# Scan outputs of all token tiles in two PSUM banks, one for each half of the heads

## The chip, the core and the metric

The kernel runs on one core of a Trainium2 chip. What counts is the device time of one execution in microseconds. TensorE (PE in the profile) multiplies matrices into PSUM, VectorE (DVE), ScalarE (ACT) and GpSimd (POOL) work element by element, SyncE (SP) issues most transfers, and the DMA engines move data between HBM and SBUF.

## The reference

The model is a backbone of two layers over 256 context tokens and 256 latent tokens, 1024 features wide. Each layer has a token mixer of four head groups (A windowed attention, B neighbourhood attention, C a gated convolution, D a gated linear recurrence that runs in both directions) and then an expert layer, which fills most of the time. The change touches only the output of group D. Its reference goes chunk by chunk:

```
attn = jnp.einsum('bhid,bhjd,bhijd->bhij', qc, kc, decay)
o = jnp.einsum('bhij,bhjv->bhiv', attn, vc) + jnp.einsum('bhid,bhdv->bhiv', qc * jnp.exp(G), S)
...
return o_f + rev(o_b), oc_f + rev(oc_b)
```

So an output is a product inside the chunk (attention weights by values) plus, for each direction, a decayed query times the state that the chunk starts from. There are four heads of 64 features.

## The kernel before

Tokens lie in four tiles of 128: tiles 0 and 1 are context, 2 and 3 latent. Layer 0 works on all four, layer 1 (the last one) mixes only the latent tiles. In group D the feature-major operands hold two heads on the 128 partitions: index ct chooses the pair of heads, hh the half of the partitions (0 to 63 or 64 to 127) on which a head lies.

The mixer of a layer is a list of named pieces, ORDERS (L58), and the function mixers runs them in that order (L856). The pieces that matter here:
- d_level:n (L740, hgrn_level) computes one level of the in-chunk weights: ScalarE, GpSimd and VectorE build operands, TensorE multiplies them into two "sc" banks, one for each half (L547), and VectorE merges them into attnT (L554). d_states (hgrn_states) carries the states from chunk to chunk: transposes (L484), products (L490), VectorE updates (L497, L500).
- d_out (L745) makes the outputs. For each token tile tt and half hh, hgrn_out's inner function o (L560) takes the one buffer with tag "o", adds for both ct the in-chunk term (128 rows deep, attnT by di) and the state terms (64 rows deep, eG by st), and VectorE copies the 128x128 result into yd (L751). Layer 0 has eight such results, layer 1 four.
- b_v, b_k, b_q, d_gate are projections: in_slab loads a weight slab, splits it into a high and a low part (L211 or L213, and L215), and mm3 (L224) runs three matmuls for each block of 128 input features. proj and wide take the result bank with tag "mm", of which there are three (self.nmm).
- a_attn:tt and b_attn:tt are attention pieces: scores in "sc" (L597), transposes in "tr" (L618), outputs in "o" (L622).

PSUM has eight banks: "sc" 2, "tr" 2, "mm" 3, "o" 1. The order written in the list is not the order on the engines: a scheduler moves instructions ahead where their operands and buffers allow. The buffers of a tag are given out in program order, so the n-th user of "mm" waits for the release of the buffer by the user three before it. In the list of layer 0 stands 'a_attn:0', 'b_q', 'd_out', 'a_attn:2', 'b_v', 'b_k'; in that of layer 1 'd_level:6', 'd_out', 'b_k', 'd_gate', 'b_v', 'b_q'. An fp32 matmul is two records in the trace.

Of the kernel before, what the change touches and what calls it, by code (L numbers as in the profile page):

```python
# [15 lines left out]
AF = mybir.ActivationFunctionType  # L16
# [5 lines left out]
P = 128  # L22
# [162 lines left out]
class Kernel:  # L185
# [370 lines left out]
    def hgrn_out(self, at, di, dirs, psp):  # L556

        nc = self.nc

        def o(tt, hh):  # L560
            po = self.t(psp, [P, 2, 64], tag="o", bufs=1)
            c = slice(tt * P, tt * P + P)
            r = slice(hh * 64, hh * 64 + 64)
            for ct in range(2):
                h = ct * 2 + hh
                terms = [(at[:, hh, tt, ct, :], di[:, tt, h * 64:h * 64 + 64])]
                for states, e in dirs:
                    if tt in states:
                        terms.append((e[r, ct, c], states[tt][r, ct, :]))
                for m, (x, y) in enumerate(terms):  # L570
                    nc.tensor.matmul(po[:, ct, :], x, y, start=m == 0, stop=m == len(terms) - 1)
            return po
        return o

    def attention(self, name, l, qT, kx, kc, v, heads, tt, y, pool, psp, mask=None, sink=None):

# [77 lines left out]
    def mixers(self, l, modt, tick=None, pre=()):  # L654
        nc, A, tc = self.nc, self.A, self.tc
        V, S, Gp = nc.vector, nc.scalar, nc.gpsimd
        last = l == DEPTH - 1
        lo = C if last else 0
        tts = list(range(lo // P, 4))
        with ExitStack() as es:  # L660
            fp = es.enter_context(tc.tile_pool(name=f"fp{l}", bufs=1))
            psp = es.enter_context(tc.tile_pool(name=f"ps{l}", bufs=2, space=PSUM))
# [48 lines left out]
            b = _Bag()  # L711
# [31 lines left out]
                self.hgrn_level(n, b.at, l, b.q, b.kd, b.Gd, fp, psp)  # L743

            def d_out():  # L745
                of = self.hgrn_out(b.at, b.di, [b.states[0], b.states[1]], psp)
                b.yd = self.t(fp, [P, 4, 256], tag="yd")
                for tt in tts:
                    yv = b.yd[:, tt, :].rearrange("p (c h d) -> p h c d", c=2, h=2)
                    for hh in range(2):  # L750
                        V.tensor_copy(yv[:, hh], of(tt, hh))  # L751

            def d_gate():
                for n, ps in enumerate(wide("dg", lo)):
# [101 lines left out]
            for piece in ORDERS[l]:  # L856
                name, _, d = piece.partition(":")
# [605 lines left out]
```

## Time and profile before

| | us |
|---|---|
| three timed runs, median | 2888.43 |
| lowest and highest | 2881.9, 2890.88 |
| the profiled execution | 2893.59 |
| its span in the trace | 2891.8 |
| TensorE busy | 2716.0 (94%) |
| VectorE busy | 2072.2 (72%) |
| ScalarE busy | 1142.5 (40%) |
| GpSimd busy | 1102.7 (38%) |
| mean granted TensorE clock | 0.967 |

The mixers run in two stretches of the span, layer 0 early (scan levels and outputs around 150 to 270 us) and layer 1 around 1800 to 1950 us. The output matmuls are at 225 to 246 us and at 1875 to 1890 us. A share of the whole span says little about them, so the rows below are taken from these stretches. [...] Matmuls overlap: one matmul's record is longer than the distance to the next, so paces are read from starts.

### The profile page before, as it was taken

To read this page: it belongs to the slowest core of one execution; us is meant where nothing else is said; L and a number is where in the kernel's file an instruction comes from. 1 tells how busy PE (TensorE), PEld (TensorE's weight loads), DVE (VectorE), ACT (ScalarE), POOL (GpSimd) and SP (SyncE) were. 2 spreads that over 40 slices of the span, in tenths; PEclk is the share of its full clock that TensorE was granted. 3 is DMA by queue.
4 is the path that set the end of the run, shared out by engine and by line. 5 is a ranking of instruction groups with operands and counts; after the bars stand their busy time and mean duration, and the time that the engine had idled before them with its cause. 6 is when DMAs were issued, how large, how long until landed. Compare 5 with 4: busy or idle time off the path is not lost.

```text
span 2891.8 us, 41509 instructions
## 1 busy us (share of the span) xinstructions
PE 2716.0 (94%) x15750; PEld 2398.9 (83%) x15750; DVE 2072.2 (72%) x3616; ACT 1142.5 (40%) x1742; POOL 1102.7 (38%) x651
## 2 busy tenths in 40 slices
PE   7799999889999999999999988999889999999998
PEld 4678788779999898888887867689889998887776
DVE  6883878999677888888878867747973315665655
ACT  4433433235533333333333334334345544444443
POOL 3531134455145344433433304425656574440000
PEclk9988999999999999999999998989999999999999
DMA  6321423347889899999989952324557776557884
GB/s 237 110 81 58 127 88 117 97 157 270 296 281 332 317 336 333 333 338 329 326 319 351 370 169 86 98 85 151 158 186 241 245 248 228 183 189 260 277 275 162
DMA packets 265784, 639.24 MB, mean 221 GB/s; under 512 B 19184, under 2 KB 136688, under 8 KB 262768
## 3 DMA queue, kind: packets, MB, share of 16 engines
q1 hardware_dynamic: 228720, 502.36, 51.4%
q0 software_dynamic: 36864, 134.23, 12.6%
q8 instruction: 123, 2.02, 0.3%
q14 instruction: 77, 0.63, 0.1%
HBM read 574.39 MB, written 62.13 MB: 220 GB/s over the span
## 4 chain that ended last, share of the span: by engine, by line
PE 32%; DVE 25%; DMA 18%; issue 9%; ACT 4%; POOL 2%; DVEq 0%; ACTq 0%; POOLq 0%; SPq 0%
DMA wraw<-in_uT_dram 12%; PE S L224 11%; PE mm L224 8%; DVE vL L215 7%; DMA ga<-spd 5%; PE pa L1307 5%; PE G L1197 5%; ACT ah L1257 2%; DVE ga L1254 2%; ACT wH L211 2%; DVE t L1046 1%; DVE wL L215 1%; DVE eq L939 1%; DVE al L1261 1%; DVE tok L1064 1%
## 5 line engine op out<-in xcount | busy, mean ns | idle before, releaser
L215 POOL TENSOR_TENSOR wL<-wraw,wH 128x1024 fp32r<-128x1024 f32 x228 | 577.3, 2535 | 739.7 <-ACT wH L211 542.7
L224 PE MATMUL S<-hH,wL 128*128 128x384 f32 (+1 forms) x2048 | 606.2, 314 | 20.6 <-POOL wL L215 13.3
L224 PE MATMUL S<-hH,wH 128*128 128x384 f32 (+1 forms) x2048 | 605.7, 314 | 5.0 <-ACT wH L211 3.2
L211 ACT ACTIVATE wH<-wraw 128x1024 fp32r<-128x1024 f32 x320 | 337.2, 1055 | 395.9 <-DMA wraw<-in_uT_dram 359.5
L224 PEld LDWEIGHTS S<-hH,wL 128*128 128x128 f32 x2048 | 393.4, 192 | 31.1 <-POOL wL L215 14.5
L1307 PE MATMUL pa<-vH,al 128*128 128x512 f32 x1280 | 399.2, 393 | 19.4 <-DVE al L1261 19.2
L224 PEld LDWEIGHTS S<-hH,wH 128*128 128x128 f32 x2048 | 393.1, 192 | 10.6 <-ACT wH L211 5.7
L1307 PE MATMUL pa<-vL,ah 128*128 128x512 f32 x1280 | 396.9, 391 | 3.2 <-DVE vL L215 2.9
L1307 PE MATMUL pa<-vH,ah 128*128 128x512 f32 x1280 | 395.6, 390 | 2.5 <-ACT ah L1257 1.8
L215 DVE TENSOR_TENSOR vL<-wraw,vH 128x1024 fp32r<-128x1024 f32 x256 | 333.3, 1332 | 66.1 <-ACT vH L211 64.8
L224 PE MATMUL S<-hL,wH 128*128 128x384 f32 (+1 forms) x2048 | 348.2, 311 | 0.0
L211 ACT ACTIVATE vH<-wraw 128x1024 fp32r<-128x1024 f32 x256 | 263.3, 1053 | 186.4 <-PE pa L1307 144.1
L224 PEld LDWEIGHTS S<-hL,wH 128*128 128x128 f32 x2048 | 312.7, 191 | 0.0
L1307 PEld LDWEIGHTS pa<-vH,al 128*128 128x128 f32 x1280 | 237.5, 188 | 81.5 <-DVE al L1261 34.0
L1013 POOL DMA_INDIRECT row<-in_v_dram,idx x128 | 188.3, 1471 | 301.9 <-DVE tok L1064 277.3
L1307 PEld LDWEIGHTS pa<-vL,ah 128*128 128x128 f32 x1280 | 238.8, 188 | 59.1 <-DVE vL L215 10.0
L1013 POOL DMA_INDIRECT row<-in_u_dram,idx x128 | 180.9, 1413 | 270.6 <-DVE score L1046 230.0
L1307 PEld LDWEIGHTS pa<-vH,ah 128*128 128x128 f32 x1280 | 238.2, 188 | 48.9 <-ACT ah L1257 2.2
L224 PE MATMUL mm<-hH,wH 128*128 128x256 f32 (+1 forms) x776 | 256.1, 349 | 9.9 <-ACT hH L362 2.5
L224 PE MATMUL mm<-hH,wL 128*128 128x256 f32 (+1 forms) x776 | 252.4, 344 | 8.6 <-DVE wL L215 8.3
L1109 ACT ACTIVATE ga<-S 128x384 f32<-128x384 f32 (+1 forms) x256 | 110.4, 432 | 332.0 <-PE S L224 331.5
L1261 DVE TENSOR_TENSOR al<-ga,ah 128x768 fp32r<-128x768 f32 (+1 forms) x128 | 137.4, 1074 | 138.0 <-ACT ah L1257 138.0
(322 smaller groups left out, 4076.4 us busy)
## 6 DMA issues: line engine op xcount, KB each, us to landing
wraw<-in_uT_dram SPq DMA_DIRECT2D x256, 512.0 KB, 4.4
wraw<-in_v_dram SPq DMA_DIRECT2D x256, 512.0 KB, 5.7
gd<-gst SPq DMA_DIRECT2D x20, 2048.0 KB, 6.7
wraw<-in_w_in_dram SPq DMA_DIRECT2D x52, 512.0 KB, 3.6
gt<-gd SPq DMA_DIRECT2D x32, 768.0 KB, 9.4
row<-in_w_modT_dram SPq DMA_DIRECT2D x48, 512.0 KB, 6.6
wraw<-in_w_modT_dram SPq DMA_DIRECT2D x32, 512.0 KB, 3.7
wraw<-in_w_q_dram SPq DMA_DIRECT2D x32, 512.0 KB, 3.7
```

The lines of the kernel that those rows point to most:

```text
L211: nc.scalar.activation(h, w, AF.Copy)
L215: e.tensor_tensor(lo, w, h.bitcast(F32), op=ALU.subtract)
L224: nc.tensor.matmul(ps, x, y, start=start and m == 0, stop=stop and m == len(seq) - 1, skip_group_check=skip)
L939: V.tensor_tensor(eq, self.iota16.unsqueeze(1).unsqueeze(1).to_broadcast(shape), rank.unsqueeze(3).to_broadcast(shape), op=ALU.is_equal)
L1013: Gp.indirect_dma_start(out=x, out_offset=None, in_=rows[n], in_offset=bass.IndirectOffsetOnAxis(ap=idx[:, k:k + 1], axis=0))
L1046: V.tensor_tensor_reduce(j, x, ht, 1.0, 0.0, op0=ALU.mult, op1=ALU.add, accum_out=a[:, k:k + 1])
L1109: self.gelu = S.activation(ga[:, e, :], ps, AF.Gelu_apprx_tanh)
L1197: nc.tensor.matmul(pg[:, t, :], Y[:, q + t, :], X[:, q + t, :], start=True, stop=True)
L1254: V.tensor_tensor(gv, gv, b.gt[:, :, g % 2 * 2:g % 2 * 2 + 2].rearrange("p b e t -> p e b t"), op=ALU.mult)
L1257: S.activation(b.ah, ga, AF.Copy)
L1261: V.tensor_tensor(b.al, b.gated, b.ah.bitcast(F32), op=ALU.subtract)
L1307: nc.tensor.matmul(pacc[tau, h], (ah, ah, al)[m][:, e, tau * P:(tau + 1) * P], vs[e][m == 1][:, h * 512:h * 512 + 512], start=g == 0 and e ...
```

## The change

Function o now takes a token tile alone. Two buffers for the whole piece, one for each half of the heads, hold the results of all four token tiles ([P, 4, 2, 64] in fp32, one bank each). They come from the tag "mm". Inside, the two halves alternate: the in-chunk terms of both halves, then for each direction the state terms of both halves. After all tiles one ScalarE instruction copies half 0 and one VectorE instruction half 1 into yd.

```diff
--- before.py
+++ after.py
@@ -557,20 +557,21 @@
 
         nc = self.nc
 
-        def o(tt, hh):
-            po = self.t(psp, [P, 2, 64], tag="o", bufs=1)
+        def o(tt):
             c = slice(tt * P, tt * P + P)
-            r = slice(hh * 64, hh * 64 + 64)
             for ct in range(2):
-                h = ct * 2 + hh
-                terms = [(at[:, hh, tt, ct, :], di[:, tt, h * 64:h * 64 + 64])]
-                for states, e in dirs:
-                    if tt in states:
-                        terms.append((e[r, ct, c], states[tt][r, ct, :]))
-                for m, (x, y) in enumerate(terms):
-                    nc.tensor.matmul(po[:, ct, :], x, y, start=m == 0, stop=m == len(terms) - 1)
-            return po
-        return o
+                live = [(states[tt], e) for states, e in dirs if tt in states]
+                for hh in range(2):
+                    h = ct * 2 + hh
+                    nc.tensor.matmul(po[hh][:, tt, ct, :], at[:, hh, tt, ct, :], di[:, tt, h * 64:h * 64 + 64], start=True,
+                                     stop=not live)
+                for m, (st, e) in enumerate(live):
+                    for hh in range(2):
+                        r = slice(hh * 64, hh * 64 + 64)
+                        nc.tensor.matmul(po[hh][:, tt, ct, :], e[r, ct, c], st[r, ct, :], start=False,
+                                         stop=m == len(live) - 1)
+        po = [self.t(psp, [P, 4, 2, 64], tag="mm", bufs=self.nmm) for _ in range(2)]
+        return o, po
 
     def attention(self, name, l, qT, kx, kc, v, heads, tt, y, pool, psp, mask=None, sink=None):
 
@@ -743,12 +744,14 @@
                 self.hgrn_level(n, b.at, l, b.q, b.kd, b.Gd, fp, psp)
 
             def d_out():
-                of = self.hgrn_out(b.at, b.di, [b.states[0], b.states[1]], psp)
+                of, po = self.hgrn_out(b.at, b.di, [b.states[0], b.states[1]], psp)
                 b.yd = self.t(fp, [P, 4, 256], tag="yd")
                 for tt in tts:
-                    yv = b.yd[:, tt, :].rearrange("p (c h d) -> p h c d", c=2, h=2)
-                    for hh in range(2):
-                        V.tensor_copy(yv[:, hh], of(tt, hh))
+                    of(tt)
+                c = slice(tts[0], 4)
+                yv = b.yd.rearrange("p t (c h d) -> p h t c d", c=2, h=2)
+                S.activation(yv[:, 0, c], po[0][:, c], AF.Copy)
+                V.tensor_copy(yv[:, 1, c], po[1][:, c])
 
             def d_gate():
                 for n, ps in enumerate(wide("dg", lo)):
```

How the order on TensorE changes at three places. Numbers after a name are running numbers of buffers.

Layer 0, in the scan levels (about 175 us). mm_1673 is a result bank of b_v, tr and sc are the states' and levels' banks. Before:

```order
L224 MATMUL mm_1673<-wL_1664,hH_290 128x256
L547 MATMUL sc_1157<-big_1141,big_1140 128x128 x3
L547 MATMUL sc_1158<-big_1141,big_1140 128x128 x3
L547 MATMUL sc_1157<-big_1141,big_1140 128x128
L547 MATMUL sc_1158<-big_1141,big_1140 128x128
L484 MATMUL tr_1214<-small_59,big_1183 128x128 x2
L224 MATMUL mm_1673<-wL_1670,hH_290 128x256 x4
L490 MATMUL tr_1219<-di_589,khT_1217 128x128
```

After, at the same place:

```order
L547 MATMUL sc_1157<-big_1141,big_1140 128x128 x3
L547 MATMUL sc_1158<-big_1141,big_1140 128x128 x3
L547 MATMUL sc_1157<-big_1141,big_1140 128x128
L547 MATMUL sc_1158<-big_1141,big_1140 128x128
L490 MATMUL tr_1193<-di_589,khT_1191 128x128 x2
L484 MATMUL tr_1201<-small_59,big_1183 128x128 x2
L547 MATMUL sc_1169<-big_1141,big_1140 128x128 x3
L547 MATMUL sc_1170<-big_1141,big_1140 128x128 x3
```

b_v's matmuls (L224) no longer stand between those of the levels; its first one stands behind the first two of d_out (L566 into mm_1526 and mm_1527).

Layer 0, d_out. o_1551 is the one output buffer, mm_1836 a projection's bank. Before, one result:

```order
L571 MATMUL o_1551<-di_589,attnT_893 128x64
L571 MATMUL o_1551<-st_1209,eG_1181 128x64
L571 MATMUL o_1551<-st_1374,eG_1333 128x64
L571 MATMUL o_1551<-di_589,attnT_893 128x64
L571 MATMUL o_1551<-st_1209,eG_1181 128x64
L571 MATMUL o_1551<-st_1374,eG_1333 128x64
L224 MATMUL mm_1836<-hH_290,wH_1832 128x512
L224 MATMUL mm_1836<-hH_290,wL_1833 128x512
```

After, from the middle of d_out; mm_1526 holds half 0 and mm_1527 half 1:

```order
L566 MATMUL mm_1526<-di_589,attnT_893 128x64
L566 MATMUL mm_1527<-di_589,attnT_893 128x64
L571 MATMUL mm_1526<-st_1209,eG_1181 128x64
L571 MATMUL mm_1527<-st_1209,eG_1181 128x64
L571 MATMUL mm_1526<-st_1374,eG_1333 128x64
L571 MATMUL mm_1527<-st_1374,eG_1333 128x64
L566 MATMUL mm_1526<-di_589,attnT_893 128x64
L566 MATMUL mm_1527<-di_589,attnT_893 128x64
```

The halves alternate between two banks, all of d_out but its first two matmuls is in one piece without projection matmuls in it, and the 'a_attn:2' transposes and outputs and the rest of b_v and all of b_k stand behind it.

Layer 1, b_k. mm_15748 is b_k's first bank, sc_15378 and sc_15379 belong to a level, sc_15397 to attention. Before, in the levels:

```order
L224 MATMUL mm_15748<-hH_14553,wH_15744 128x512
L224 MATMUL mm_15748<-hH_14553,wL_15745 128x512
L224 MATMUL mm_15748<-hH_14553,wH_15744 128x512
L224 MATMUL mm_15748<-hH_14553,wL_15745 128x512
L547 MATMUL sc_15378<-dq_15002,big_15375 128x128 x4
L224 MATMUL mm_15748<-hL_14554,wH_15744 128x512 x2
L547 MATMUL sc_15379<-dq_15002,big_15375 128x128 x4
L597 MATMUL sc_15397<-ak_15140,aq_15067 128x512
L224 MATMUL mm_15748<-hL_14554,wH_15744 128x512 x3
```

After, the end of d_out (mm_15696 is half 0, mm_15697 half 1) and the first matmuls of b_k (mm_15732):

```order
L566 MATMUL mm_15697<-di_14753,attnT_15228 128x64
L571 MATMUL mm_15697<-st_15328,eG_15287 128x64
L571 MATMUL mm_15696<-st_15648,eG_15620 128x64
L571 MATMUL mm_15697<-st_15648,eG_15620 128x64
L566 MATMUL mm_15696<-di_14753,attnT_15228 128x64
L566 MATMUL mm_15697<-di_14753,attnT_15228 128x64
L571 MATMUL mm_15696<-st_15328,eG_15287 128x64
L571 MATMUL mm_15697<-st_15328,eG_15287 128x64
L571 MATMUL mm_15696<-st_15648,eG_15620 128x64
L571 MATMUL mm_15697<-st_15648,eG_15620 128x64
L224 MATMUL mm_15732<-hH_14541,wH_15728 128x512
L224 MATMUL mm_15732<-hH_14541,wL_15729 128x512
```

All of b_k's 48 matmuls of 512 columns, and 21 of the gate's, which were spread over the levels, now stand behind d_out. In d_out itself the two halves alternate only in the last eight matmuls; ahead of these come runs with one half alone, in which 128-row and 64-row terms follow one another. On VectorE two weight steps of b_k's second slab (L213, L215), which stood between the state updates, stand behind the output copy, and two group-norm steps of A (L637) stand ahead of it.

## Rows read from the trace of the kernel before

**Rows 1.** Page, part 1: busy us, share of the span, instructions of each engine.

```profile
PE 2716.0 (94%) x15750; PEld 2398.9 (83%) x15750; DVE 2072.2 (72%) x3616; ACT 1142.5 (40%) x1742; POOL 1102.7 (38%) x651
```

**Rows 2.** Stretches in layer 0: length, busy PE, PEld, DVE, ACT, POOL, PEclk, DMA share, GB/s.

```profile
172.00:195.00 23.00, 21.41 (x176) 18.98 (x174) 20.54 (x36) 4.73 (x8) 6.55 (x4) 0.95 0.19 58
195.00:224.00 29.00, 29.00 (x165) 20.34 (x164) 26.91 (x63) 13.67 (x36) 4.02 (x3) 1.00 0.49 155
...
242.00:257.00 15.00, 15.00 (x59) 13.19 (x58) 1.01 (x3) 1.20 (x2) 0.00 (x0) 0.52 0.00 1
257.00:270.00 13.00, 11.69 (x36) 6.73 (x36) 4.09 (x12) 5.09 (x13) 3.42 (x3) 0.64 0.26 81
```

**Rows 3.** PE groups by form, 171.9 to 195 us: busy us, mean ns, idle before.

```profile
L224 PE MATMUL mm<-wH,hH 128*128 128x256 f32 x23 | 6.1, 296 | 0.0
...
L224 PE MATMUL mm<-wL,hH 128*128 128x256 f32 x16 | 2.7, 293 | 0.0
```

**Rows 4.** Stretches in layer 1, columns as in rows 2.

```profile
1818.00:1842.00 24.00, 21.14 (x119) 14.16 (x117) 23.28 (x53) 5.27 (x10) 13.42 (x17) 0.93 0.39 125
1842.00:1875.00 33.00, 30.97 (x225) 24.00 (x221) 21.48 (x56) 17.65 (x44) 13.89 (x28) 1.00 0.14 46
1875.00:1890.00 15.00, 15.00 (x64) 13.23 (x64) 2.51 (x7) 1.06 (x1) 0.00 (x0) 0.58 0.05 20
1895.00:1911.00 16.00, 16.00 (x136) 15.87 (x134) 5.83 (x8) 5.60 (x13) 5.77 (x4) 1.00 0.40 125
```

**Rows 5.** PE groups by form, 1818.5 to 1874.9 us, columns as in rows 3.

```profile
L224 PE MATMUL mm<-hH,wH 128*128 128x512 f32 x16 | 7.3, 454 | 0.0
...
L224 PE MATMUL mm<-wH,hH 128*128 128x256 f32 x8 | 2.1, 296 | 0.0
```

**Rows 6.** Who waited for the output matmuls of line 571: us, times.

```profile
  DVE yd L751: 25.5, 12
```

**Rows 7.** ACT groups by form, 225 to 260 us, columns as in rows 3.

```profile
L620 ACT ACTIVATE PT<-tr 128x512 f32<-128x512 f32 x4 | 2.4, 598 | 20.7 <-PE o L622 18.9 <-PE tr L618 1.8
```

**Rows 8.** Chain of waits, 1868 to 1912 us: start, us, what.

```profile
1869.71 0.69 DVE wH L213
...
1871.69 1.22 DVE wL L215
...
1874.99 0.80 PE o L571 x4
...
1890.39 20.64 PE mm L224 x155
1911.03 1.05 PE sc L597 x3
```

**Rows 9.** Timeline of PE, 237.9 to 247 us: start, us, instructions.

```profile
237.91 0.33 PE L571 MATMUL o<-di,attnT 128*128 128x64 f32 x2
238.17 0.66 PE L571 MATMUL o<-st,eG 64*128 64x64 f32 x4
238.75 0.43 PE L571 MATMUL o<-di,attnT 128*128 128x64 f32 x2
239.12 0.66 PE L571 MATMUL o<-st,eG 64*128 64x64 f32 x4
239.70 0.50 PE L224 MATMUL mm<-hH,wH 128*128 128x512 f32 x1
...
244.02 1.11 PE L571 MATMUL o<-st,eG 64*128 64x64 f32 x4
245.06 0.69 PE L571 MATMUL o<-di,attnT 128*128 128x64 f32 x2
245.68 1.11 PE L571 MATMUL o<-st,eG 64*128 64x64 f32 x4
```

**Rows 10.** Chain of waits, 1828 to 1831 us, columns as in rows 8.

```profile
1829.74 1.10 PE sc L547 x16
```

**Rows 11.** Timeline of DVE, 1868 to 1915 us, columns as in rows 9.

```profile
1876.03 0.34 DVE L637 TENSOR_SCALAR ya<-ya,rg 128x256 f32<-128x256 f32 x1
```

## What I predicted, and why

> **What bounds the kernel now.** I read the page's busy times first: TensorE is busy 94% of the span [rows 1], so a microsecond of its work that is added counts, and one that another engine saves counts only where TensorE is idle. The scan outputs stand in two places, one for each layer, and I read each as a row of stretches. In layer 0 [rows 2], 172 to 195 us is the tail of the scan levels: VectorE is busy 20.54 of 23.00 us and sets the pace, and TensorE's 21.41 us hold 61 projection matmuls of b_v that fill its gaps (22, 23 and 16; two of the three groups are in [rows 3]). From 195 to 224 TensorE is busy 29.00 of 29.00. In layer 1 [rows 4], 1818 to 1842 is again VectorE's (23.28 of 24.00), 1842 to 1875 is shared, and from 1875 TensorE has no idle time. The fill there is 48 matmuls of b_k, 512 columns wide (three groups of 16), and 21 of the gate slab, 256 wide (8, 8 and 5); one group of each is in [rows 5]. Last I read the waits on the output matmuls: VectorE's copies wait 25.5 us for them, 12 times, with one "o" bank to go through [rows 6]. That is idle time of an engine that does not bound these stretches. TensorE meanwhile fills them with projection matmuls, so the wait itself is worth nothing to the end.
>
> **Part 1, copies.** Twelve VectorE copies go; two of each layer come, one on ScalarE. A 128x512 ScalarE copy out of PSUM takes 598 ns [rows 7]. Behind d_out TensorE has dense projection work with operands that are there, which hides the copies in both layers. In layer 0 one stands ahead of a_attn:2's probability copies on ScalarE, and TensorE's transposes there now stand behind d_out: +0.6 us if nothing covers it, which I count. In layer 1 nothing: 155 projection matmuls stand behind it [rows 8].
>
> **Part 2, d_out on TensorE.** An fp32 matmul runs as two passes, and layer 0 has 80 passes (32 of the 128-row term, 48 of the 64-row terms), layer 1 has 48 (16 and 32). The prices are in the timeline [rows 9]. At the full clock four 64-row passes take 238.17 to 238.75 = 0.58 us and two 128-row passes 0.37. Two equations, with a for a pass and b for a change of height: 4a + b = 0.58, 2a + b = 0.37, so a = 0.105, b = 0.16. At the low clock 1.04 and 0.62 give a = 0.21, b = 0.20. Where two matmuls use different halves of the rows and different banks, the levels show the price: 16 passes in 1.10 us [rows 10], 0.069 each. Layer 0 before: four outputs of 12 passes at 1.79 us (237.91 to 239.70) and four of 8 passes at 0.42 less, 1.37; together 12.6 us at the full clock. After: 32 x 0.105 + 48 x 0.069 + 16 x 0.16 = 9.3 us. So **-3.3 us**. In layer 1 the order shows that the scheduler does not keep the halves side by side at first: fourteen changes of height are left, and most neighbours write one bank. I take no pairing: 48 x 0.105 + 14 x 0.16 = 7.3 us at the full clock, 48 x 0.21 + 14 x 0.20 = 12.9 at the low one.
>
> The trace shows pairs of halves running faster in two banks, 0.069 against 0.105 us [rows 9, 10], and also what those banks are otherwise for: the fill of [rows 3, 5] accumulates in "mm" banks. [...]
>
> **Part 3, the two banks.** This is the largest term. The new tiles take two of the three "mm" banks, and buffers of a tag are given in program order. In the lists d_out stands before b_v (layer 0) and b_k (layer 1). Those projections used to be pulled forward into the gaps of the levels; now they cannot have a bank before d_out has its two, and the order shows them behind it.
>
> Layer 0: a 256-column projection matmul at the full clock passes in 16.00 / 136 = 0.118 us (1895 to 1911, [rows 4]). 61 x 0.12 = **+7.3 us** of TensorE work leaves gaps where it was nearly free and goes where TensorE is full. The levels get shorter by at most the idle time VectorE has there, 23.00 - 20.54 = 2.5 us [rows 2]; I take **-2** (0 to -2.5). [...] Layer 0 sums to 7.3 - 2 - 3.3 + 0.6 = **+2.6** (-5 to +12).
>
> Layer 1 can be summed whole. Before, from the first output matmul to the first score matmul: 1874.99 to 1911.03 = 36.04 us [rows 8], of which d_out with 16 projection matmuls among it takes 15.40 and 155 projection matmuls 20.64; these should take 155 x 0.118 = 18.3, so the low clock still cost them 2.3. After: d_out 10.1 us (the middle of 7.3 and 12.9, since 1875 to 1890 was granted 0.58 [rows 4]); 48 wide ones at twice 0.118, 11.3; 155 + 16 + 21 = 192 narrow ones, 22.7; and 2.3 of low clock. That is 46.4, **+10.4 us**. The start moves: two weight steps on VectorE (0.69 and 1.22 us [rows 8]) now stand behind the output copy, -1.9; two group-norm steps of 0.34 [rows 11] stand ahead, +0.7. The levels lose their fill: VectorE has 0.7 us idle in 1818 to 1842 [rows 4], so of the shortening I take -1 (0 to -3). Layer 1: 10.4 - 1.9 + 0.7 - 1 = **+8.2** (+1 to +19: d_out at 7.3 and no low clock after it, -5.1, with the full -3, at the lower end; d_out at 12.9 and the levels, now with wider gaps, in part at the low clock, at the upper: TensorE works 21.14 + 30.97 = 52.11 us in them, and a sixth of it at half the speed and uncovered costs another 8).
>
> On the clock the trace shows 0.58 in 1875 to 1890 although TensorE was busy 15.00 of 15.00 us [rows 4]. [...]
>
> **Sum.** +2.6 + 8.2 = +10.8 us. The profiled execution took 2893.59 us (span 2891.8), so by it 2904.4. It lies above all three timed runs (2881.9 to 2890.88, median 2888.43); against the median the same sum gives 2899.2, and I say **2899**, +0.37%. A measurement of this kernel tells about 0.3% (8.7 us) from no change.
>
> **Rivals.** *The gains cancel the fill* (the same, chance 0.34): d_out in layer 1 runs at the full clock, 7.3 us instead of 10.1, the projections behind it lose nothing (-2.3), and in layer 0 the low clock comes for a shorter time (-3): 10.8 - 2.8 - 2.3 - 3 = +2.7, so 2891. For it: the pairing price of [rows 10] is real. Against it: the 0.58 and 0.52 of [rows 2, 4], both in just these matmuls.
> *The clock stays up* (faster, chance 0.13; the other side): the lower clock in both layers was due to d_out's slow alternation of heights and same-bank passes, and goes with them. Layer 0 then gets back the 11.9 us and the whole 2.5 of its levels, layer 1 ends at its lower bound: 2.6 - 11.9 - 0.5 = -9.8, and +1; 2879.6. This side holds, too, a shortening of layer 1's levels beyond the 3 us, if TensorE and not VectorE sets the pace of 1842 to 1875. It decides if the granted clock is above 0.9 from d_out to the following scores in both layers. Against it: in layer 1 the passes are not paired.
> *It does not do what it says*: the two halves are not side by side in layer 1. The order shows this already, and it is in the sum; pairing 32 passes would be worth 32 x 0.036 = 1.2 us.
> *Worse*: the levels without fill run at the low clock; 2899 + 8, up to 2913 with layer 0's bound in part. This belongs to the forecast's side.
>
> **How the numbers follow.** The forecast, slower with displaced fill, has 0.53, its dearer form with the levels at the low clock among it. Faster by over 0.3% 0.13, within 0.3% 0.34, slower 0.53. The range, 2881 to 2913, reaches over the second case whole and leaves out most of the third, and of the dearer form what lies past +24.
>
> **What would show it.** Each step has its place. In layer 0: no 256-wide projection matmuls between the last levels, 61 more behind d_out, and d_out in one piece of about 9 us. In layer 1: 48 wide and 192 narrow projections between d_out and the first scores, some 46 us from the first output matmul, against 36. The copies: under 1 us of wait on them. It is wrong if the levels become shorter by as much as the fill that left them, which would mean that TensorE and not VectorE set their pace; or if the granted clock in the two d_outs and behind them is near 1.

## The result: slower by 1.2%

| | before | changed |
|---|---|---|
| timed runs, median, us | 2888.36 | 2925.24 |
| lowest and highest | 2881.9, 2890.88 | 2912.14, 2926.56 |
| span of the profiled execution | 2891.8 | 2924.8 |
| ratio, 95% interval | | 1.0117 (1.0085 to 1.0149) |

These are four runs of each kernel. I had said 2899, and 2881 to 2913. The direction was right and the size was not: 36.9 us between the medians and 33.0 between the spans, against 10.8. An execution can run long at a lower granted clock (one of the twelve of fill_kept below took 3013.97 us at a mean clock of 0.833); the ratios compare the others.

The page's first part, for the kernel changed [rows 1 for before]: TensorE is busy 16.6 us longer on the same 15750 matmul records, in a span that is 33.0 us longer, so half of the loss is idle time of TensorE.

```profile
PE 2732.6 (93%) x15750; PEld 2411.6 (82%) x15750; DVE 2073.2 (71%) x3606; ACT 1144.8 (39%) x1744; POOL 1104.0 (38%) x651
```

The place is layer 1. These are its stretches in the kernel changed (length, busy PE, PEld, DVE, ACT, POOL, PEclk, which is the granted TensorE clock as a share of full speed, DMA share, GB/s); the first three answer to [rows 4].

```profile
1818.00:1842.00 24.00, 15.31 (x80) 10.75 (x76) 20.30 (x40) 2.65 (x6) 11.21 (x13) 0.62 0.32 99
1842.00:1875.00 33.00, 26.17 (x99) 17.42 (x96) 11.53 (x39) 13.24 (x32) 9.93 (x24) 0.50 0.08 25
1875.00:1890.00 15.00, 14.05 (x67) 12.31 (x65) 7.64 (x16) 4.95 (x11) 6.06 (x11) 0.50 0.13 35
...
1896.00:1908.00 12.00, 11.20 (x46) 9.68 (x48) 1.93 (x3) 0.00 (x0) 0.00 (x0) 0.50 0.00 0
...
1914.00:1944.00 30.00, 30.00 (x223) 28.69 (x222) 9.43 (x12) 10.56 (x19) 8.48 (x5) 1.00 0.31 96
```

The column to look at is the clock. Before, 1842 to 1875 was granted 1.00; now the scan levels from 1824 us on and d_out are granted 0.50, half of full speed, and VectorE, from whose idle time I had worked out how far the levels could shorten, is busy only 11.53 of 33.00 us. It waits. The same TensorE work by form shows where the time goes. First the kernel before, 1823 to 1875 us (busy us, mean ns, idle before), then the kernel changed, 1823.8 to 1896.5:

```profile
L547 PE MATMUL sc<-big,big 64*128 64x128 f32 x80 | 8.3, 299 | 0.4 <-DVE big L538 0.4
L622 PE MATMUL o<-av,PT 128*128 128x64 f32 x64 | 7.8, 275 | 0.0
L597 PE MATMUL sc<-ak,aq 64*128 64x512 f32 x16 | 7.2, 641 | 0.8 <-DVE rm L598 0.8
...
L618 PE MATMUL tr<-small,big 128*128 128x128 f32 x32 | 4.7, 280 | 0.2 <-ACT big L605 0.2
```

```profile
L623 PE MATMUL o<-av,PT 128*128 128x64 f32 x64 | 14.9, 421 | 0.0
L547 PE MATMUL sc<-big,big 64*128 64x128 f32 x80 | 14.7, 458 | 6.0 <-DVE big L538 6.0
L598 PE MATMUL sc<-ak,aq 64*128 64x512 f32 x16 | 11.6, 1137 | 1.4 <-DVE rm L599 1.0 <-DVE attnT L554 0.4
L619 PE MATMUL tr<-small,big 128*128 128x128 f32 x32 | 8.7, 426 | 0.0
```

The same counts take 49.9 us instead of 28.0. To split the loss I use three marks of layer 1: A, the first VectorE merge into attnT (L554); B, the first output matmul; C, the first score matmul of group B (sc<-dk,dk). In the timeline they start at 1823.83, 1874.99 and 1910.96 before; in the kernel changed at 1825.24, and:

```profile
1896.80 0.69 PE L566 MATMUL mm<-di,attnT 128*128 128x64 f32 x2 [0.92 <-DVE attnT L554]
...
1908.42 0.79 PE L224 MATMUL mm<-hH,wH 128*128 128x512 f32 x1
...
1944.52 1.13 PE L598 MATMUL sc<-dk,dk 64*128 64x512 f32 x4
```

So A to B went from 51.16 to 71.56 us (+20.4), B to C from 35.97 to 47.72 (+11.75), together +32.2 of the 33.0 in the span. Before A the two executions are 1.4 us apart.

Layer 0, the rows that answer to [rows 2]:

```profile
172.00:195.00 23.00, 20.83 (x124) 16.79 (x124) 20.17 (x37) 3.29 (x6) 2.52 (x3) 0.71 0.17 53
195.00:224.00 29.00, 28.74 (x190) 21.90 (x190) 23.39 (x63) 13.99 (x41) 1.05 (x2) 1.00 0.34 105
242.00:257.00 15.00, 13.64 (x57) 9.59 (x55) 11.24 (x13) 2.82 (x5) 7.75 (x4) 1.00 0.45 148
257.00:270.00 13.00, 12.81 (x58) 10.25 (x58) 2.27 (x9) 5.29 (x14) 0.90 (x2) 0.61 0.31 113
```

The same mark C stands at 252.87 us against 257.26, so nothing is lost there in this execution. The low clock stands elsewhere than before: in the levels, 172 to 195, the clock is 0.71 instead of 0.95, and in 242 to 257 it is 1.00 instead of 0.52.

The copies wait, as before, on the output matmuls (compare [rows 6]; who waited for line 571, us, times), and nobody waits on them:

```profile
  ACT yd L753: 20.7, 2
  DVE yd L754: 17.5, 2
```

### The profile page after: what moved, and what is told of

Read it like the earlier page. It is cut to its first block, busy times and chain, and to the rows that moved or that the text cites. A ratio compares the mean times of both kernels' runs of the same rounds, so it can differ in the third digit from the quotient of the medians.

```text
span 2924.8 us, 41507 instructions
## 1 busy us (share of the span) xinstructions
PE 2732.6 (93%) x15750; PEld 2411.6 (82%) x15750; DVE 2073.2 (71%) x3606; ACT 1144.8 (39%) x1744; POOL 1104.0 (38%) x651
## 5 line engine op out<-in xcount | busy, mean ns | idle before, releaser
L215 POOL TENSOR_TENSOR wL<-wraw,wH 128x1024 fp32r<-128x1024 f32 x228 | 577.1, 2534 | 740.0 <-ACT wH L211 590.5
L224 PE MATMUL S<-hH,wL 128*128 128x384 f32 (+1 forms) x2048 | 605.7, 314 | 20.6 <-POOL wL L215 11.7
L224 PE MATMUL S<-hH,wH 128*128 128x384 f32 (+1 forms) x2048 | 606.2, 314 | 7.0 <-ACT wH L211 5.5
L224 PEld LDWEIGHTS S<-hH,wL 128*128 128x128 f32 x2048 | 393.4, 192 | 30.2 <-DVE wL L215 14.9
L224 PEld LDWEIGHTS S<-hH,wH 128*128 128x128 f32 x2048 | 393.4, 192 | 13.3 <-ACT wH L211 9.0
L215 DVE TENSOR_TENSOR vL<-wraw,vH 128x1024 fp32r<-128x1024 f32 x256 | 333.4, 1332 | 66.1 <-ACT vH L211 65.0
L224 PE MATMUL S<-hL,wH 128*128 128x384 f32 (+1 forms) x2048 | 347.2, 310 | 0.0
L224 PEld LDWEIGHTS S<-hL,wH 128*128 128x128 f32 x2048 | 311.3, 190 | 0.0
L224 PE MATMUL mm<-hH,wH 128*128 128x256 f32 (+1 forms) x776 | 255.8, 349 | 9.1 <-ACT hH L362 2.8
L224 PE MATMUL mm<-hH,wL 128*128 128x256 f32 (+1 forms) x776 | 251.5, 343 | 9.7 <-DVE wL L215 9.4
L215 DVE TENSOR_TENSOR wL<-wraw,wH 128x1024 fp32r<-128x1024 f32 x128 | 157.8, 1240 | 126.5 <-ACT wH L211 122.2
```

Source lines behind the costliest of these rows:

```text
L215: e.tensor_tensor(lo, w, h.bitcast(F32), op=ALU.subtract)
L224: nc.tensor.matmul(ps, x, y, start=start and m == 0, stop=stop and m == len(seq) - 1, skip_group_check=skip)
```

## The experiments

My theory after this reading: the two banks drive the projections out of layer 1's levels; without them the clock falls, and the low clock makes the levels long. The rivals: the long-lived tiles with their order of matmuls cost it; or the new order on the other engines makes the levels long; or layer 0 has a share. All ratios below are to the kernel before on the same chip, with 95% intervals.

**Layer 0 alone (l0_only).** d_out_new and d_out_old are d_out as changed and as before.

```diff
+            def d_out():
+                (d_out_new if l == 0 else d_out_old)()
```

> Layer 0 as in the changed kernel, layer 1 as before. In the trace of the changed kernel the experts of layer 0 start some 3 to 5 us earlier than before, and layer 1 loses the rest. Theory (all of the loss is in layer 1): 2884 to 2888 us, the same as before or a little under it. Rival (my prediction's sum: layer 0 costs 2.6 us, up to 12): 2891 to 2900.

Ratio 1.0019 (0.9989 to 1.0049), median 2891.37 us. The median lies in the rival's range and not in the theory's, but the interval, some -3 to +14 us, holds zero as well as the 2.6: it excludes the whole loss of 33 us from layer 0 and decides nothing between the two. A to C in layer 0, by the same marks, took 119.58, 112.95 and 107.05 us in three executions with the old layer 0 (before, l1_old_in_mm and l1_sc_only), and 111.97, 111.99, 117.46, 117.48, 117.89 and 119.62 in six with the new one. The means are 2.9 us apart, and the old ones alone spread over 12.5; my +2.6 lies within what these can tell, and so does zero.

**The old d_out, in projection banks (l1_old_in_mm).**

```diff
-            po = self.t(psp, [P, 2, 64], tag="o", bufs=1)
+            po = self.t(psp, [P, 2, 64], tag="mm", bufs=self.nmm) if l else self.t(psp, [P, 2, 64], tag="o", bufs=1)
```

> The kernel before, with one edit: in layer 1 the four single results of d_out take their bank from the three projection banks. No pairing, still four results and four VectorE copies; by the order the projections' matmuls leave the scan levels as in the changed kernel. Theory (the loss comes from the fill leaving the levels, and the lower clock there): the granted clock is near 0.50 through the levels (about 1824 to 1895 us) and the time is 2915 to 2930 us. Rival (the two long-lived tiles and their order of matmuls cost it): 2888 to 2897, clock near 1 in the levels.

Ratio 1.0117 (1.0068 to 1.0166), median 2917.14: the whole loss, with no pairing, no long-lived tile and the old copies. Its row of the levels (columns as above):

```profile
1813.00:1881.00 68.00, 56.57 (x232) 41.18 (x230) 32.47 (x88) 18.95 (x45) 19.26 (x37) 0.50 0.11 35
```

A to B takes 71.52 us and B to C 48.95, against 71.56 and 47.72 in the kernel changed. From B to C the two-bank form is 1.2 us shorter than this one, in one execution of each; where the banks come from accounts for the loss.

**The changed d_out, with b_k ahead of it in the list of layer 1 (l1_bk_first).**

```diff
-'d_level:6', 'd_out', 'b_k', 'd_gate'
+'d_level:6', 'b_k', 'd_out', 'd_gate'
```

> The changed kernel with one edit: in the list of layer 1 b_k stands ahead of d_out, so that its two slabs get their banks first and their 48 matmuls of 512 columns stay in the levels. d_out keeps its two banks, its pairing and its two copies. Theory (fill and clock): the levels run at a granted clock of 0.9 or more as before, layer 1 takes as long as before or up to 3 us less, 2880 to 2890 us. Rival (the two-bank d_out itself is what costs): 2910 to 2926.

Ratio 1.0033 (1.0003 to 1.0063), median 2890.86, just above what was expected. A to B is back at 51.29 us and B to C at 36.98, and the clock in the levels at 0.97:

```profile
1810.00:1860.00 50.00, 43.68 (x272) 31.36 (x272) 37.63 (x96) 20.65 (x48) 20.86 (x37) 0.97 0.23 71
```

So the rival of the long-lived tiles falls as the cause of the 1.2%: they are all still there. Some 0.3% is left; A to C in layer 1 shows 1.1 us of it, and where the rest arises is not shown. Compare the count of matmul records, 272 in 50 us here and 232 in 68 us above.

**More TensorE work in the levels: each score twice (l1_twice).**

```diff
+                        for _ in range(2 if l else 1):
-                        nc.tensor.matmul(pg[hh][:, tt, ct, :], KB[r, ct, c], Q[r, ct, c], start=True, stop=True)
+                            nc.tensor.matmul(pg[hh][:, tt, ct, :], KB[r, ct, c], Q[r, ct, c], start=True, stop=True)
```

> The changed kernel with one edit: in layer 1 each score matmul of the scan levels is issued twice in a row, with the same result; nothing else moves, the projections stay behind d_out. It adds 16 matmuls (32 records) a level, 112 in all. Theory (the clock makes the levels long): if the extra work keeps the clock at the upper level in part of the levels, the levels get shorter than the 73 us of the changed kernel although TensorE has more to do, and the time is 2895 to 2920 us; if the clock stays at 0.50, each level gets longer by up to 2 us, 2930 to 2940 us, and nothing is told of the order. Rival (the new order on VectorE, ScalarE and GpSimd makes the levels long, not the clock): 2925 to 2940 us with a clock near 1.

Ratio 1.0165 (1.0115 to 1.0214), median 2929.35. The edit added 128 records (15878 against 15750), 16 a level, which is half of what the expectation counts. By its own terms it tells little of the order: the clock stayed low in most of the levels, and A to B took 75.62 us.

```profile
1824.00:1841.00 17.00, 13.09 (x75) 11.11 (x75) 10.06 (x23) 1.77 (x4) 5.88 (x10) 0.50 0.29 98
1841.00:1848.00 7.00, 4.34 (x14) 1.79 (x14) 4.64 (x17) 1.72 (x5) 0.00 (x0) 0.99 0.11 37
1848.00:1896.00 48.00, 45.12 (x209) 36.42 (x208) 17.46 (x45) 15.88 (x37) 12.47 (x28) 0.50 0.04 11
```

It shows, though, that TensorE was busy 45.12 of 48.00 us at a granted clock of 0.50, all but 8 of the 209 records being 64 or 128 columns wide. And the clock came up twice, to 0.99 in 1841 to 1848 and to 1.00 in 1896 to 1902, without any projection in the levels. Ahead of each stand 32 records of one level's doubled scores in one piece:

```profile
1836.28 4.34 PE L548 MATMUL sc<-dq,big 64*128 64x128 f32 x32 [0.74 <-DVE attnT L555]
...
1889.57 4.38 PE L548 MATMUL sc<-big,big 64*128 64x128 f32 x32
```

```profile
1896.00:1902.00 6.00, 4.52 (x40) 3.55 (x39) 4.12 (x12) 0.38 (x1) 0.00 (x0) 1.00 0.02 6
```

**Wide matmuls in the place of the lost fill (l1_dummy).** This one leaves the projections behind d_out and gives the levels as many wide matmuls to no purpose.

```diff
+            for m in range(3 if l else 0):
+                nc.tensor.matmul(pg[m % 2].rearrange("p a b t -> p (a b t)"), self.ident, k[0][:, 0, :], start=True, stop=True)
```

> The changed kernel with one edit: in layer 1 each scan level first issues three matmuls of 512 columns into its own two score banks, which the level's scores then overwrite; 24 in all, 48 records, as many as b_k's matmuls that left the levels. The real b_k stays behind d_out. Theory (without the fill the clock falls and that makes the levels long): the granted clock in the levels is back near 1, the levels take about 55 to 60 us instead of 73, and the whole is 2895 to 2905 us, what my prediction's sum gave with the clock up. Rival (the order on the other engines makes the levels long): they take 73 us or more with the clock at 1, 2925 to 2945 us. If the clock stays at 0.50 in spite of the fill, some 22 us come on top, about 2945, and the clock's cause is open.

Ratio 1.0056 (1.0033 to 1.0079), median 2901.56: a loss of 0.56% where the kernel changed lost 1.17%, some 18 us less, with 48 wide matmul records more. The levels, A to B, take 54.84 us, at a clock of 0.94 and 1.00; then d_out at 0.55:

```profile
1827.00:1855.00 28.00, 23.93 (x132) 14.82 (x132) 13.84 (x40) 6.71 (x16) 7.85 (x15) 0.94 0.13 43
1855.00:1882.00 27.00, 23.56 (x145) 15.00 (x144) 18.83 (x52) 12.18 (x29) 10.45 (x23) 1.00 0.06 20
1882.00:1892.00 10.00, 10.00 (x49) 8.69 (x49) 0.45 (x2) 0.18 (x1) 0.00 (x0) 0.55 0.01 2
```

The sequences on ScalarE and GpSimd around A to C are those of the kernel changed but for a step or two, and those on VectorE but for some that trade places or stand ahead of A. So it isn't the new order of the other engines that makes the levels long: with the clock up they are within 3.7 us of before. What is left of the loss is +10.4 us from B to C (46.33 against 35.97), the stretch of the displaced fill and d_out, which I had at +10.4. How long the levels would be with the clock up and no fill at all, no run shows.

**Two other banks in layer 1 (l1_sc).**

```diff
-        po = [self.t(psp, [P, 4, 2, 64], tag="mm", bufs=self.nmm) for _ in range(2)]
+        po = [self.t(psp, [P, 4, 2, 64], tag="sc") if l else self.t(psp, [P, 4, 2, 64], tag="mm", bufs=self.nmm) for _ in range(2)]
```

> The changed kernel with one edit: in layer 1 the two output banks are the two score banks instead of two of the three projection banks. By the order b_k and most of the gate's matmuls are back in the levels, and d_out keeps its two banks and two copies. Theory: 2880 to 2892 us, clock near 1 in the levels, layer 1 within 3 us of before. Rival (the two long-lived output banks cost, whichever they are): 2910 to 2926.

Ratio 0.9979 (0.9962 to 0.9996), median 2885.99. A to B 51.30 us, B to C 31.63, which is 4.3 us less than before. Its rows of d_out and of the projections behind it:

```profile
1876.00:1886.00 10.00, 9.99 (x52) 8.63 (x53) 1.86 (x5) 0.25 (x1) 0.00 (x0) 0.66 0.08 29
1886.00:1908.00 22.00, 22.00 (x170) 21.81 (x171) 6.84 (x10) 8.79 (x18) 8.48 (x5) 0.92 0.30 93
```

The output matmuls take 9.3 us from first to last here (1876.01 to 1885.30) instead of 15.0, and the low clock in them is shorter. Of the 15.0, 16 projection records among them took 3.8 us; here three take 0.6. The score banks are idle between the levels and B's scores (before, no matmul into them starts between 1871.8 and 1910.9), so nothing is driven out.

**The lists of both layers changed, banks as in the changed kernel (fill_kept).**

```diff
-'b_q', 'd_out', 'a_attn:2', 'b_v', 'b_k'
+'b_q', 'b_v', 'd_out', 'a_attn:2', 'b_k'
...
-'d_level:6', 'd_out', 'b_k', 'd_gate'
+'d_level:6', 'b_k', 'd_out', 'd_gate'
```

> The changed kernel with both lists edited: in layer 0 b_v stands ahead of d_out, in layer 1 b_k, so that these projections have their banks first and fill the levels as before. Theory: what is left of the change is the pairing in layer 0 (3.3 us by the sum) and little in layer 1 (0 to 3 us): 2882 to 2889 us, the same as before within the measurement, or a little under it. Rival (layer 0 gained by having its fill moved behind d_out): a few us more than with layer 1's list alone, 2890 to 2896.

Ratio 1.0012 (0.9995 to 1.0029), median 2890.15; in layer 1 A to C is 87.55 us against 87.13 before. The loss is gone, and no gain is left that can be told. The median stands just above the theory's range, at the rival's lower end, and the interval overlaps with that of l1_bk_first: what layer 0's list is worth isn't told.

**The score banks with two forms of layer 0 (l1_sc_only, sc_bv).** The first takes the old d_out in layer 0 (its edit is shown), the second the new one with b_v ahead of it.

```diff
+        po = [self.t(psp, [P, 4, 2, 64], tag="sc") for _ in range(2)]
...
+            def d_out():
+                (d_out_new if l == 1 else d_out_old)()
```

> Layer 0 as before; in layer 1 the two output banks are the two score banks, with the alternating halves and the two copies. Theory (in layer 1 the change is worth 4 us once it takes no projection bank; layer 0's form is worth nothing that can be told): 0.996 to 0.9995 of before, 2877 to 2887 us, as with layer 0 changed too. Rival (the gain of the kernel with the score banks came from layer 0): ratio 1.000 or above.

> Layer 1 with the score banks, layer 0 with the two projection banks but b_v ahead of d_out in the list, so that both layers keep the fill of their scan levels. Theory: the 4 us of layer 1, and up to 5 us in layer 0, where the stretch from the first level to B's first scores took 100.3 us with this list against 102.4 to 107.3 without: 0.995 to 0.999 of before, 2874 to 2885 us. Rival (layer 0's stretch swings by the clock alone): as with the score banks alone, 0.998.

Ratios 0.9980 (0.9951 to 1.0009) and 0.9981 (0.9954 to 1.0009), medians 2881.68 and 2882.92. B to C is 31.63 and 30.19 us. Three kernels with the score banks in layer 1 thus read 0.998, one of them with an interval clear of 1: this form of the change gains about 0.2%, the 4 to 6 us of its B to C, which is close to what these measurements can tell. What layer 0 is given makes no difference that shows. The 100.3 and 102.4 to 107.3 us of the second expectation were counted from a merge that is not the same in all kernels; from the first merge the list with b_v ahead takes 112.21 (fill_kept) and 108.81 us (sc_bv), against 111.97 to 119.62 without.

## Why the prediction was wrong in size

**Copies: right.** The trace shows nobody waiting on them, and with the old copies l1_old_in_mm loses the same.

**d_out on TensorE: the prices right, the totals near.** In layer 0 of the kernel changed, the later tiles' four 128-row passes and eight paired 64-row passes take turns, first at the full clock, then at the low one:

```profile
220.38 0.44 PE L571 MATMUL mm<-st,eG 64*128 64x64 f32 x4
...
224.20 0.66 PE L571 MATMUL mm<-st,eG 64*128 64x64 f32 x8
224.79 0.66 PE L566 MATMUL mm<-di,attnT 128*128 128x64 f32 x4
225.38 0.66 PE L571 MATMUL mm<-st,eG 64*128 64x64 f32 x8
...
227.69 1.11 PE L566 MATMUL mm<-di,attnT 128*128 128x64 f32 x4
228.74 1.12 PE L571 MATMUL mm<-st,eG 64*128 64x64 f32 x8
229.79 1.97 PE L619 MATMUL tr<-small,big 128*128 128x128 f32 x8
```

Eight paired passes take 224.20 to 224.79 = 0.59 us; 8 x 0.069 alone makes 0.55. All but the first four passes stand in one piece of 9.4 us (220.38 to 229.79). I had 9.3 (the sum makes 9.2) at the full clock, and the last 3 us (226.8 to 229.8) were granted 0.50, so that the totals agree is in part luck. In layer 1 d_out took 1896.80 to 1908.42 = 11.6 us, where I had 10.1 between 7.3 and 12.9: it was granted 0.50 throughout, and the last passes were paired.

**The displaced fill: right in layer 1.** Layer 0's fill left the levels (seven narrow projection records in 172 to 195 us instead of 61); what that cost, a forecast +2.6 us in sum, the runs can't tell from zero. In layer 1 B to C grew by 11.75 us against the 10.4 of the sum, and by 10.4 in l1_dummy, with the clock up in the levels. Of the 47.72 us, 36.1 stand behind d_out (1908.42 to 1944.52); the sum had 36.3.

**The levels of layer 1 without their fill: the step that failed.** I wrote that the levels lose their fill and took -1 us, which with the start's -1.9 and +0.7 makes -2.2 for A to B, and bounded the other side at +8, a sixth of TensorE's work at half the speed (a sixth of 52.11 is 8.7). A to B was +20.4: the clock was at 0.50 from 1824 to 1912 us, all of the levels from A on and not a sixth. l1_dummy shows it from the one side (fill of no use, clock at 0.94 and 1.00, levels 54.84 us) and l1_old_in_mm from the other (no fill, clock at 0.50, 71.52 us, with the old d_out). The mechanism stood in my text as the dear form of the forecast, so the term was mis-sized, not missing. Two rows could have warned me. In 1875 to 1890 [rows 4] output matmuls, with 16 projection records among them, ran at 0.58 with TensorE busy all the time, and the levels without the projections are mostly matmuls of 64 or 128 columns; whether the width has to do with the clock, no run separates. And in the kernel before TensorE was busy 30.97 of the 33.00 us in 1842 to 1875, VectorE 21.48: TensorE, with its fill, was nearer to setting the pace there, so its speed mattered and not VectorE's idle time alone. I had called that stretch shared, and yet took the shortening of all the levels from VectorE's 23.28 of 24.00 in the stretch ahead.

**The rivals.** Gains that cancel the fill: no; layer 1's d_out was granted 0.50. A clock that stays up: in layer 1 the opposite came. With the banks taken elsewhere, though (l1_sc), the low clock in d_out is shorter (0.66 in 1876 to 1886) and B to C is 4.3 us shorter than before; how much of this is the pairing and how much the clock, no run separates. The 11.9 us that the second rival gets back in layer 0 are 15 x 0.48 + 13 x 0.36 from the clocks of [rows 2], and the first of the two, some 7 us, stands to each side in layer 0's range; no run shows that term. What the kernel changed showed there is a clock of 1.00 in 242 to 257 with 0.71 in the levels and 0.61 in 257 to 270, and mark C 4.39 us earlier in its one execution.

On where the two banks come from the runs put a number: 1.0117 with the projections' banks (l1_old_in_mm, and the kernel changed as a whole) and 0.9979 with the score banks in layer 1 (l1_sc).

## What to carry to other kernels

Before giving a new tile a bank of a shared pool, see who uses that pool to fill gaps, and whether a bank of another pool is idle then: here the change loses 1.2% with layer 1's two banks from one pool and nothing with them from the other. The fill in layer 1's levels did its own work there, and the clock in the levels was 0.97 with it (l1_bk_first) and 0.50 without it (l1_old_in_mm), so price its removal with the whole stretch at the lower clock as the bound. Where two engines look busy, ask for each stretch on its own which of them sets the pace at the other clock.

## What the runs showed of the hardware

The clock fell at the start of layer 1's levels in the kernel before too; what differs is that it came back. Before, TensorE was idle 2.46 us of 1824 to 1830, the wide projections of b_k followed, and the clock was at 1.00 from 1830 on:

```profile
1824.00:1830.00 6.00, 3.54 (x15) 2.78 (x16) 5.68 (x16) 0.38 (x1) 0.49 (x1) 0.72 0.30 119
1830.00:1836.00 6.00, 6.00 (x43) 4.05 (x39) 5.79 (x11) 1.00 (x2) 4.58 (x8) 1.00 0.28 87
```

In the kernel changed it fell at 1823.8 us, after a stretch in which TensorE was busy 3.39 of 6.00 us, and did not come back although TensorE was then busy 6.00 of 6.00 in stretches; it came back at 1912.6, with projections 512 columns wide running back to back from 1908.42:

```profile
1818.00:1824.00 6.00, 3.39 (x31) 2.63 (x28) 6.00 (x10) 2.27 (x5) 6.00 (x8) 0.99 0.29 91
1824.00:1830.00 6.00, 2.60 (x10) 1.91 (x10) 5.58 (x13) 0.38 (x1) 1.91 (x2) 0.50 0.41 131
...
1848.00:1854.00 6.00, 6.00 (x32) 5.07 (x31) 1.68 (x4) 1.80 (x5) 2.31 (x7) 0.50 0.01 3
1854.00:1860.00 6.00, 6.00 (x21) 4.17 (x22) 0.70 (x2) 1.20 (x2) 2.06 (x6) 0.50 0.00 0
...
1908.00:1914.00 6.00, 6.00 (x22) 4.75 (x21) 0.42 (x1) 0.39 (x1) 0.00 (x0) 0.62 0.00 0
```

TensorE had been idle 2.46 us just before the first of these falls and 0.94 us just before the second. There is no idle time where the clock was 0.58 inside the old d_out (1875 to 1890, TensorE busy 15.00 of 15.00 us, [rows 4]), and in the long stretches at 0.50 TensorE was mostly busy (73.23 of the 88 us from 1824 to 1912 in the kernel changed, 45.12 of 48.00 in l1_twice). So what makes it fall is not shown. What brings it back stays open too: it rose during wide projections in the kernel changed, was at 0.94 and 1.00 with wide matmuls to no purpose in l1_dummy, and in l1_twice came up to 0.99 and 1.00, each time after a piece of 32 doubled score records, and was at 0.50 again after the first.

The kernel before ran from 2862 to 2908 us over the rounds of these experiments. Differences of this size can arise outside the mixers: the profiled execution of l1_bk_first ended 29 us ahead of that of before, of which 14.6 stood at mark A (1809.21 against 1823.83), and its stretch A to C gave nothing. The marks of layer 1 inside one trace, such as A to C, told effects of a few us apart that the total times did not.
